# A two-layer encoder trunk: the odd layer's side work in woven streams of steps, and two recurrence chains that take their steps together

## Chip, cores and metric

One core of one Trainium2 chip runs the whole program in one launch. The metric is device time in microseconds (us), the median of several runs. The kernel before takes 2757.74 us, the median of 3 runs (2757.59 to 2758.05).

## What is computed

Two consecutive encoder layers over a sequence of 2048 rows of 1024 columns, fp32. The even layer mixes neighbourhood attention with a gated recurrence (GLA); the odd layer, which the change is mostly about, mixes HGRN2 heads with Mamba-2 (SSD) heads. Cut to the odd layer:

```python
def layer(x, c):                                   # both layers
    h = x * (1.0 + scale) + shift                  # from c
    y = odd_mixer(h, ...)                          # or even_mixer
    return layer_norm(ALPHA * x + gate * y)
def odd_mixer(h, w_in, ...):
    cq, cf_f, cf_b, ci, cg, dz, dxbc, dt_f, dt_b = split_cols(h @ w_in)
    # HGRN2: 4 heads of 128, forward and backward
    lf = logaddexp(log(lb), log1p(-lb) + log_sigmoid(cf)); k = (1 - lb) * sigmoid(-cf)
    oc = bidir_gated_recurrence(cq * 128 ** -0.5, ci, k_f, lf_f, k_b, lf_b)
    yc = rms_norm(oc) * silu(cg)
    # SSD: 8 heads of 64, 2 groups with a state of 128
    xs, bm, cm = split_cols(silu(conv1d(dxbc, conv_w, width=4) + conv_b))
    dt = softplus(dt_raw + dt_bias); a = dt * -exp(a_log)
    y = ssd(xs * dt_f, a_f, bm, cm) + rev(ssd(rev(xs * dt_b), rev(a_b), rev(bm), rev(cm))) + d_skip * xs
    yd = rms_norm(y * silu(dz))
    return concatenate([yc, yd]) @ w_out
```

## The kernel before

**In-projection.** Every fp32 product is made of three fp32r matmuls (high part by high, low by high, high by low: `hH,wh`, `hL,wh`, `hH,wl`). The in-projection of the odd layer goes unit by unit of 256 weight columns: `ci0 ci1` (values), `qf0` to `qf3` (queries and forward gates), `b0 b1` (backward gates), `x0` to `x3` (the input of the convolution), `g0 g1` and `dz0 dz1` (output gates). Each is done for the second half of the sequence ("half 1"), then for the first ("half 0"). `InProj.block` (matmuls in L205) is 24 matmuls into one PSUM bank: 128x512 in most units, 128x256 in `ci` and `dz`. The evacuations write an `st` tile on ACT or DVE (L348 to L354 for the first kind, L371 and L372 for the second), and DMAs store it to DRAM; `loading` (L184 to L186) loads and splits the next weights.

**Side work of the odd layer, per segment of 512 rows.**
- `Rec.pass_a` (L441 to L567) is the local part of one HGRN2 head: it loads the gates (`Kp`, L652), takes their sigmoid on ACT (`F`, L654), then goes through seven levels, on each of which PE makes 16 small `fine` matmuls (`blocks`, L435) or an `l` one (L498), DVE multiplies `Q` and `Kp` (L508, L510), POOL multiplies the other half of `Kp` (L512). Then come transposes `pk` (L527), the state updates `pu` (L538), a scan on DVE (L579) and the outputs `po` (L556, L561). Its generator yields 12 or 13 times. `pass_b` (L584 to L638, called `other`) adds the second direction for two heads.
- `Ssd.conv` (L1016 to L1043) filters one of 8 channel blocks: load `cvx` (L1027), one ACT pass (L1029), three DVE passes over `cva` (L1031), a sigmoid (ACT, L1032), a product (POOL, L1033); blocks below 6 are turned on PE (`cvt`, L1039), copied on ACT (L1041) and stored as rows of `xtok` (L1042).
- `Ssd.backward` (L1045) runs a chain of 16 chunks from the last to the first. For each: store the state `sb` (L1051), load `tk` from `xtok` (L1054), weight it on POOL (L1065), two PE matmuls `pu` (L1069), decay the state on POOL (L1077), add `pu` on DVE (L1078).
- `Ssd.steps` (L975) makes the decays from `dt_raw`.

**What sets the order.** A list scheduler orders all instructions ahead of time by priority, which is the order in which the program writes them; each engine then runs its list in order. In `trunk` the side work is written whole between `units(...)` calls, each piece inside `tc.high_priority(offset=2000)`, which moves its instructions ahead by 2000 places. Heads are taken one after another, and of a head the second segment (`sg` 2 half + 1) before the first. The even layer's GLA runs two chains through `lagging` (L309): chain a leads by 6 steps, after that `mixed` takes one step of each in turn. After the in-projection follow the SSD's `local` and `forward` parts with the out-projection (L1546 to L1568, matmuls `oo` in L921).

Of the kernel before, what the change touches and what calls it, by code (L numbers as in the profile page):

```python
# [10 lines left out]
F32 = mybir.dt.float32  # L11
# [296 lines left out]

def lagging(a, b, lag):  # L309

    for _ in range(lag):
        next(a)
        yield
    yield from mixed(a, b)


def chained(*gs):
    for g in gs:
        yield from g
# [627 lines left out]
class Ssd:  # L947
# [27 lines left out]
    def steps(self, pool, tp, bank, dt_raw, half):  # L975

        e, nc = self.e, self.e.nc
        n = NC // 2
        hs = slice(half * n, (half + 1) * n)
        dt = self.dt[:, hs]  # L980
        bc = lambda r: r.unsqueeze(1).broadcast_to([P, n, 16])
        z = tp[:, 0]
        nc.vector.tensor_tensor(z, dt_raw[:, hs], bc(self.row), ALU.add)
        ab = tp[:, 1]
        nc.scalar.activation(ab, z, AF.Abs)
        nc.scalar.activation(ab, ab, AF.Exp, scale=-1.0)
# [12 lines left out]
        nc.vector.scalar_tensor_tensor(dt, z, 0.0, h, ALU.max, ALU.add)
        a = z  # L1000
        nc.vector.tensor_tensor(a, dt, bc(self.nea), ALU.mult)
        nc.scalar.copy(self.aHr[:, hs], a)
        nc.vector.tensor_tensor(self.aL[:, hs], a, self.aH[:, hs], ALU.subtract)

        for nm, m, d in (("kf", "gt", 0), ("qf", "le", 0), ("kb", "lt", 1), ("qb", "ge", 1)):
            pt = bank("sp")
            nc.tensor.matmul(pt[:, :n * 8], e.tri[m], a[:, :, d * 8:(d + 1) * 8], start=True, stop=True)
            t = self.ed[nm][:, hs]
            nc.scalar.activation(t, pt[:, :n * 8].rearrange("p (c h) -> p c h", h=8), AF.Exp)
            if nm[0] == "k":  # L1010
                nc.vector.tensor_tensor(t, t, dt[:, :, d * 8:(d + 1) * 8], ALU.mult)
        pt = bank("sp")
        nc.tensor.matmul(pt[:, :n * 16], e.ones, a.rearrange("p c h -> p (c h)"), start=True, stop=True)
        nc.scalar.activation(self.tot[:, hs].rearrange("p c h -> p (c h)"), pt[:, :n * 16], AF.Exp)

    def conv(self, pool, bank, sg, xbc, cw, cb):  # L1016

        e, nc = self.e, self.e.nc
        t0 = sg * SW
        lo, hi = max(t0 - 2, 0), min(t0 + SW + 1, S)  # L1020
        for i in range(8):
# [23 lines left out]
    def backward(self, c, pool, bank):  # L1045

        nc = self.e.nc
# [4 lines left out]
        if c:  # L1052
            tk = pool.tile([P, 768], F32, name="tk", tag="tk", bufs=2)
            nc.sync.dma_start(tk, self.tok[c * P:(c + 1) * P, :])  # L1054
            pu = self.update(c, 1, tk, tk[:, 512:], pool, bank, tk[:, :512].rearrange("p (h q) -> p h q", h=8))
            new = pool.tile([P, 512], F32, name="sb", tag="sb", bufs=2)
            self.step(new, self.sb, c, 1, pu)
            self.sb = new

    def update(self, c, d, x, b, pool, bank, xw=None):  # L1060
# [59 lines left out]
    def forward(self, c, pool, bank):  # L1120
# [22 lines left out]
            nc.vector.tensor_tensor(h8(t), h8(po), eq, ALU.mult)  # L1143
            nc.gpsimd.tensor_tensor(acc, acc, t, ALU.add)
        if c < NC - 1:
            pu = self.update(c, 0, tk, tk[:, 512:], pool, bank)
# [66 lines left out]
def trunk(ctx, tc, i, out):  # L1213
# [246 lines left out]
        U[f"x{h}"]["evac"] = ch_evac(e, xbc[2 * h:2 * h + 2], [C, C], [1.0, 1.0])  # L1460
    recs = [Rec(e, mp, mps, [(0, P, cg[h], y[h * P:(h + 1) * P])], hg, 1.0, 1, f"h{h}") for h in range(4)]

    def hgrn(h, half):
        for sg in (2 * half + 1, 2 * half):
            with tc.high_priority(offset=2000):
                run(recs[h].pass_a(sg, hgrn_prep(e, mp, cq[h], cz[h], lb[:, h:h + 1], ub[:, h:h + 1]),
                                   v_loader(e, mp, ci[h // 2][:, (h % 2) * P:(h % 2 + 1) * P], P), sg % 2))

    sd = Ssd(e, sg_, dz, y[512:1024])

    def conv(sg):
        with tc.high_priority(offset=2000):
            sd.conv(kp, xbank, sg, xbc, cw, cbias)

    def back(sg):
        for c in range(4 * sg + 3, 4 * sg - 1, -1):
            with tc.high_priority(offset=2000):
                sd.backward(c, kp, xbank)

    def steps(half):  # L1480
        with tc.high_priority(offset=2000):
            sd.steps(sp, mp.tile([P, 4, NC // 2, 16], F32, name="dtt", tag="KT", bufs=1), xbank, dt_raw, half)

    def btags(t, par):
        return {"qul": (("F", "Kp")[t], 2), "stwb": ((("stw", "kd"), ("q", "KT"))[t][par], 1), "sq": (f"S32{t}", 1),
# [3 lines left out]
        return mps.tile([P, 512], F32, name=name, tag="rg" if name == "pob" else "sd", bufs=2)  # L1489

    def other(h, sg, tags=None):
        with tc.high_priority(offset=2000):
            run(pass_b(e, recs[h:h + 2], sg, mp, bbank, tags or [btags(t, sg % 2) for t in range(2)]))

    w1 = ip.load(U["b0"])
    for g in range(2):
# [5 lines left out]
    hgrn(0, 1)  # L1502
    units("qf1", 1)
    hgrn(1, 1)
    units("ci1 qf2 b1", 1)
    hgrn(2, 1)
    units("qf3", 1)
    hgrn(3, 1)
    units("x0 x1 x2 x3", 1)
    sd.prepare(sp, i["dt_bias"], i["a_log"], i["d_skip"])  # L1510
    steps(1)
    conv(3)
    back(3)
    units("g0 g1", 1)
    run(ip.turn(U["dz0"], U["dz1"], 1, U["qf0"], U["b0"], 0, lambda n: mp.tile([P, 4, 2 * P], F32, name="xt", tag=f"T{n % 2}", bufs=1), banks(mps, "rg", 2)))
    units("ci0", 0)
    hgrn(0, 0)
    units("qf1", 0)
    hgrn(1, 0)
    units("g0 ci1", 0)  # L1520
    steps(0)
    units("x0 x1 x2 x3", 0)
    for sg in range(4):
        other(0, sg)
    conv(2)
    back(2)
    conv(1)
    units("qf2", 0)
    back(1)
    units("b1", 0)  # L1530
    conv(0)
    units("qf3", 0)
    hgrn(2, 0)
    hgrn(3, 0)
    back(0)
    units("g1", 0)
    late = []
    late.append((U["dz0"], ip.load(U["dz0"])))
    run(ip.blocks(*late[-1], 0, 0))
    late.append((U["dz1"], ip.load(U["dz1"])))  # L1540
    run(ip.blocks(*late[-1], 0, 0))
    other(2, 0)
    for u, w in late:
        run(ip.blocks(u, w, 0, 1))
# [17 lines left out]
    for c in range(NC):  # L1562
        if 0 < c < NC - 1:
            sd.local(c + 1, mp, sbank)
        if c % 4 == 1 and c < 12:
            other(2, c // 4 + 1, ftags)
# [63 lines left out]
```

## Time and profile before

| what | value |
|---|---|
| median of 3 runs | 2757.74 us |
| the profiled execution | 2761.07 us, of it in the span 2759.3 us |
| PE busy, its weight loads (PEld) | 94%, 77% of the span |
| DVE, ACT, POOL busy | 52%, 40%, 47% |
| chain that ended last, by engine | PE 64%, DVE 12%, DMA 10%, ACT 5%, issue 4%, POOL 4% |
| even layer | 0 to 1394.6 us |
| odd layer to the first `g1` matmul of half 0 | 1394.6 to 2237.8 us |
| its `g1` and `dz` units of half 0 | 2237.8 to 2362.8 us |
| change-over | 2362.8 to 2415.9 us |
| SSD outputs and out-projection | 2415.9 to 2759.3 us |

The profiled execution lies 1.8 us above its own span and 3.3 us above the median. The stretches are cut at the first `oqf0` matmul, the first `g1` matmul of half 0, the end of the last `dz` matmul and the first `oo` matmul. A busy PE is not PE at its peak, since matmuls are pipelined. The trace shows each plain fp32 matmul (the small ones) as two records.

### The profile page before, as it was taken

How to read it: one execution, taken by the hardware profiler on the slowest of the kernel's cores; microseconds unless marked ns; L12 is line 12 of the kernel's file. 1: busy time of each engine (PE TensorE's matmuls, PEld its weight loads, DVE VectorE, ACT ScalarE, POOL GpSimd, SP SyncE). 2: the span in 40 equal slices, each digit the busy share in tenths (PEclk: the TensorE clock that was granted, in tenths of full speed). 3: DMA queues.
4: the chain of work that ended last, by engine and by line, in shares of the span. 5: the costliest groups of instructions: out<-in, count | busy, mean ns of one | idle time of the engine just before them, and what ended most of it. 6: DMA issues, size and time to landing. Idle time of an engine off the chain costs nothing.

```text
span 2759.3 us, 52948 instructions
## 1 busy us (share of the span) xinstructions
PE 2585.7 (94%) x21112; PEld 2122.1 (77%) x21112; DVE 1425.6 (52%) x2343; ACT 1107.0 (40%) x2317; POOL 1302.2 (47%) x1289
## 2 busy tenths in 40 slices
PE   7999798999999999999899999999999988788988
PEld 5878687987878677777788877888787768676876
DVE  6223335124442545554545445453545468778987
ACT  3152333155344533343232333353334344645643
POOL 4252324244442434343355555244535487577775
PEclk9999999999999779999999999999999999898999
DMA  8535434323365554545455334353346666544341
GB/s 272 166 107 166 139 122 139 106 90 114 118 224 178 192 176 154 180 151 157 134 179 198 112 120 142 112 184 126 118 140 219 191 187 220 191 138 140 100 133 68
DMA packets 260999, 420.92 MB, mean 153 GB/s; under 512 B 21232, under 2 KB 138896, under 8 KB 260752
## 3 DMA queue, kind: packets, MB, share of 16 engines
q1 hardware_dynamic: 260752, 417.53, 47.1%
q8 instruction: 167, 2.74, 0.4%
q14 instruction: 80, 0.66, 0.1%
HBM read 285.07 MB, written 132.38 MB: 151 GB/s over the span
## 4 chain that ended last, share of the span: by engine, by line
PE 64%; DVE 12%; DMA 10%; ACT 5%; issue 4%; POOL 4%; SPq 1%; POOLq 0%; DVEq 0%; ACTq 0%
PE oo L921 9%; PE ox L205 5%; PE oqf L205 5%; PE nay L825 4%; DMA adw<-in_ada_w_dram 3%; PE nas L802 3%; PE obv L205 3%; PE oag L205 3%; PE oav L205 3%; PE oak L205 3%; PE og L205 2%; PE fine L435 2%; PE napt L818 2%; PE oci L205 2%; DVE w L1115 2%
## 5 line engine op out<-in xcount | busy, mean ns | idle before, releaser
L186 POOL TENSOR_TENSOR wl<-wraw,wh 128x1024 fp32r<-128x1024 f32 (+2 forms) x116 | 291.8, 2533 | 313.4 <-ACT wh L185 308.8
L921 PE MATMUL oo<-wo,yH 128*128 128x512 f32 x1024 | 326.3, 405 | 6.6 <-ACT yH L905 4.7
L512 POOL TENSOR_TENSOR Kp<-Kp,T 128x256 f32<-128x256 f32 x144 | 118.6, 824 | 238.6 <-PE l L498 70.0
L921 PEld LDWEIGHTS oo<-wo,yH 128*128 128x128 f32 x1024 | 192.4, 192 | 50.4 <-ACT yH L905 7.5
L921 PE MATMUL oo<-wo,yL 128*128 128x512 f32 x512 | 200.4, 406 | 1.9 <-DVE yL L906 1.8
L815 POOL TENSOR_TENSOR nap<-nap,nasm 128x384 f32<-128x384 f32 (+2 forms) x128 | 110.9, 896 | 188.7 <-DVE nasm L810 152.8
L185 ACT CAST wh<-wraw 128x1024 fp32r<-128x1024 f32 (+2 forms) x116 | 116.8, 1051 | 158.0 <-PE obqk L205 25.8
L510 DVE TENSOR_TENSOR Kp<-Kp,T 128x256 f32<-128x256 f32 x144 | 106.6, 740 | 122.0 <-PE fine L435 59.3
L508 DVE TENSOR_TENSOR Q<-Q,T 128x512 f32<-128x512 f32 x144 | 140.9, 979 | 0.0
L825 PE MATMUL nay<-napts,nav 128*64 128x128 f32 (+1 forms) x896 | 134.8, 299 | 2.7 <-DVE napts L821 2.1
L825 PEld LDWEIGHTS nay<-napts,nav 128*64 128x64 f32 (+1 forms) x896 | 104.8, 148 | 36.8 <-issue 25.4
L1031 DVE SCALAR_TENSOR_TENSOR cva<-cvx,cw,cva 128x512 f32<-128x512 f32 x96 | 90.2, 952 | 62.3 <-ACT cva L1029 60.9
L921 PEld LDWEIGHTS oo<-wo,yL 128*128 128x128 f32 x512 | 98.1, 192 | 26.5 <-DVE yL L906 4.4
L473 DVE COPY_PREDICATED S<-lmask,fine 128x128 f32<-128x128 int32 x160 | 43.8, 298 | 122.6 <-PE fine L435 122.2
L205 PE MATMUL oqf<-hH,wh 128*128 128x512 f32 x256 | 102.5, 401 | 4.9 <-ACT st L353 4.9
L205 PE MATMUL oqf<-hH,wl 128*128 128x512 f32 x256 | 102.0, 399 | 0.0
L205 PE MATMUL ox<-hL,wh 128*128 128x512 f32 x256 | 101.9, 398 | 0.0
L205 PE MATMUL ox<-hH,wl 128*128 128x512 f32 x256 | 101.8, 398 | 0.0
L205 PE MATMUL oqf<-hL,wh 128*128 128x512 f32 x256 | 101.8, 398 | 0.0
L205 PE MATMUL ox<-hH,wh 128*128 128x512 f32 x256 | 101.7, 397 | 0.0
L807 ACT ACTIVATE nap<-nap,namx 128x384 f32<-128x384 f32 (+2 forms) x128 | 79.3, 620 | 54.6 <-DVE namx L805 53.4
L805 DVE CUSTOM_DVE_ANT_0 nap<-nas,nat 128x384 f32<-128x384 f32 (+2 forms) x128 | 70.4, 557 | 51.8 <-PE napt L818 33.0
(377 smaller groups left out, 7657.5 us busy)
## 6 DMA issues: line engine op xcount, KB each, us to landing
wraw<-in_o_w_dram SPq DMA_DIRECT2D x56, 512.0 KB
wraw<-in_e_w_dram SPq DMA_DIRECT2D x44, 512.0 KB
adw<-in_ada_w_dram SPq DMA_DIRECT2D x32, 512.0 KB
tk<-xtok SPq DMA_DIRECT2D x31, 384.0 KB
nat<-in_na_tab_dram SPq DMA_DIRECT2D x16, 640.0 KB
xt<-in_x_dram SPq DMA_DIRECT2D x16, 512.0 KB
adw<-in_ada_p_dram SPq DMA_DIRECT2D x16, 512.0 KB
r<-in_x_dram SPq DMA_DIRECT2D x16, 512.0 KB
```

The source lines that it names most:

```text
L185: nc.scalar.copy(h[:, sl], raw)
L186: (nc.vector if e.wl_dve else nc.gpsimd).tensor_sub(l[:, sl], raw, h[:, sl].bitcast(F32))
L205: nc.tensor.matmul(oo, a, b, start=d == 0 and m == 0, stop=d == ND - 1 and m == 2)
L508: nc.vector.tensor_tensor(qv, qv, view(tcur, toff + 1, [[nb - 1, 2], [2, n2], [0, s]]), ALU.mult)
L510: nc.vector.tensor_tensor(kv, kv, view(tcur, toff + nb + 1, [[2, n2], [0, s]]), ALU.mult)
L512: nc.gpsimd.tensor_tensor(kv, kv, view(tcur, toff, [[2, n2], [0, s]]), ALU.mult)
L802: nc.tensor.matmul(sc[:, :nk], a[sl, qs], b[sl, ks[0], ks[1]], start=m == 0, stop=m == 2, tile_position=(p0, 0))
L807: nc.scalar.activation(p[:, :nk], p[:, :nk], AF.Exp, bias=mx[:, n:n + 1], scale=-1.0, accum_out=sm[:, n:n + 1])
L815: nc.gpsimd.tensor_tensor(p[:, :nk], p[:, :nk], sm[:, n:n + 1].broadcast_to([P, nk]), ALU.mult)
L825: nc.tensor.matmul(yp[sl, n, :], vs[:4 * w, n, b, p0:p0 + 64], pts[:4 * w, b, :], start=b == 0, stop=b == nb - 1, tile_position=(0, p0))
L921: nc.tensor.matmul(o, a[:, c, :], b[c][:, ns], start=c == order[0] and m == 0, stop=c == order[-1] and m == 2)
L1031: nc.vector.scalar_tensor_tensor(acc, xr[:, k:k + SW], cw[:, i, k:k + 1], acc, ALU.mult, ALU.add)
```

## The change

1. `lagging` lets its two chains take a step each in one go and then yields twice (which keeps the number of yields); before, `mixed` yielded between them.
2. A new `woven(front, *streams)` runs the projection's steps and, whenever the number of front steps reaches a stream's due count (`first`, then every `per`), one step of that stream. In the odd layer the recurrences are one stream and the SSD's steps, convolution and backward chain another. `high_priority` is gone.
3. `hgrn` takes a list of heads and runs the two segments of a half as two chains through `lagging`, 6 steps apart.
4. `conv` takes several segments and goes block by block through all of them; a block's transposes and stores come one item late. Of `backward`, the weighting and the update become two steps. The tile `dtt` moves to another pool.
5. The order of units in half 0 is now `ci0 qf1 ci1 g0 qf2 b1 qf3 x0 x1 x2 x3 g1`, then `dz`; before, the `x` units stood ahead of `qf2`. In half 1 the order of units stays.

```diff
 def lagging(a, b, lag):
     for _ in range(lag):
         next(a)
         yield
-    yield from mixed(a, b)
+    alive = [a, b]
+    while alive:
+        for g in list(alive):
+            if next(g, alive) is alive:
+                alive.remove(g)
+        yield
+        if len(alive) == 2:
+            yield
...
+def woven(front, *streams):
+    due = [first for _, first, _ in streams]
+    for j, _ in enumerate(front):
+        for x, (g, _, per) in enumerate(streams):
+            while due[x] <= j:
+                due[x] += per
+                next(g, None)
+    for g, _, _ in streams:
+        run(g)
...
+        for i in range(8):
+            for sg in sgs:
+                done.append(filtered(i, sg))
+                if len(done) > 1:
+                    put(*done.pop(0))
+                yield
+        put(*done.pop(0))
+        yield
...
-            pu = self.update(c, 1, tk, tk[:, 512:], pool, bank, tk[:, :512].rearrange("p (h q) -> p h q", h=8))
+            xw = self.weighted(c, 1, tk, pool, tk[:, :512].rearrange("p (h q) -> p h q", h=8))
+            yield
+            pu = self.update(xw, tk[:, 512:], bank)
...
-    def hgrn(h, half):
-        for sg in (2 * half + 1, 2 * half):
-            with tc.high_priority(offset=2000):
-                run(recs[h].pass_a(sg, hgrn_prep(e, mp, cq[h], cz[h], lb[:, h:h + 1], ub[:, h:h + 1]),
-                                   v_loader(e, mp, ci[h // 2][:, (h % 2) * P:(h % 2 + 1) * P], P), sg % 2))
+    def hgrn(hs, half):
+        def chain(sg):
+            for h in hs:
+                yield from recs[h].pass_a(sg, hgrn_prep(e, mp, cq[h], cz[h], lb[:, h:h + 1], ub[:, h:h + 1]),
+                                          v_loader(e, mp, ci[h // 2][:, (h % 2) * P:(h % 2 + 1) * P], P), sg % 2)
+        return lagging(chain(2 * half + 1), chain(2 * half), Rec.STEPS // 2)
...
+    woven(chained(steps_of("qf1 ci1 qf2 b1 qf3 x0 x1 x2 x3 g0 g1", 1), turn),
+          (hgrn(range(4), 1), 0, 2), (chained(steps(1), conv(3), back(3)), 90, 8))
     units("ci0", 0)
...
+    def last():
+        yield from steps_of("qf1 ci1 g0 qf2 b1 qf3 x0 x1 x2 x3 g1", 0)
...
+        for nm in ("dz0", "dz1"):
+            late.append((U[nm], ip.load(U[nm])))
+            yield from ip.blocks(*late[-1], 0, 0)
+        for u, w in late:
+            yield from ip.blocks(u, w, 0, 1)
+    woven(last(), (chained(hgrn(range(2), 0), *(other(0, sg) for sg in range(4)), hgrn(range(2, 4), 0), other(2, 0)), 0, 2.15),
+          (chained(steps(0), conv(2, 1, 0), back(2, 1, 0)), 122, 2.67))
```

Three places show how the lists of the engines move.

On PE, in the unit `qf2` of half 1, a recurrence's `fine` and `pu` matmuls stood in turn, one by one, in the list before:

```order
L205 MATMUL oqf_15289<-hL,wh 128x512
L205 MATMUL oqf_15289<-hH,wl 128x512
L205 MATMUL oqf_15289<-hH,wh 128x512
L435 MATMUL fine<-Q,km 32x32 x10
L538 MATMUL pu<-v,KT 128x128
L435 MATMUL fine<-Q,km 32x32
```

and so on, `fine` and `pu` by turns, 14 pieces in all. Now they stand in runs, with projection matmuls (`oqf`) between them:

```order
L548 MATMUL pk<-c_ident,Kp 128x128 x8
L205 MATMUL oqf_14815<-hH,wl 128x512
L205 MATMUL oqf_14815<-hH,wh 128x512
L456 MATMUL fine<-Q,F 32x32 x16
L559 MATMUL pu<-v,KT 128x128 x4
L205 MATMUL oqf_14815<-hL,wh 128x512
```

From the first `oqf0` matmul to the first `g1` of half 0, the changes from one kind of small matmul to another fall from 145 to 76 (those between `fine` and `pu` or `po` from 98 to 19), and the visits from the projection to small matmuls rise from 139 to 146. The counts of matmuls stay.

On ACT, before, in the units `b1` and `qf3` of half 0: the sigmoids of head 2's gates (`F<-Kp`) stand ahead of an evacuation (`st<-ob`) of the unit `b1`, which makes those heads' backward gates:

```order
L1029 ACTIVATE cva<-cvx,cbias,cw 128x512 x2
L1041 COPY cvtt<-cvt 128x512
L1032 ACTIVATE cvx<-cva 128x512
L654 ACTIVATE F<-Kp 128x512 x2
L185 CAST wh<-wraw 128x1024 x2
L353 ACTIVATE st<-ob_21431 128x512
```

Now the sigmoids of head 2 stand in the `x` units, after the units `b1` and `qf3`:

```order
L1037 ACTIVATE tot<-sp 128x128
L648 ACTIVATE sq,ss<-opl 128x128 x2
L675 ACT_TABLE_LOAD
L675 ACTIVATE F<-Kp 128x512 x2
L676 ACTIVATE Kp<-Kp 128x1024
L1071 COPY cvtt<-cvt 128x512
L1056 ACTIVATE cva<-cvx,cbias,cw 128x512
L374 ACTIVATE st<-ox_20897 128x512
```

Nothing of the projection that still makes gates of head 2 stands behind them any more.

On PE in the `dz` units of half 0, steps of the backward chain (`pu<-tk`) were three before, the first of them here:

```order
L205 MATMUL odz_23010<-wl,hH 128x256
L205 MATMUL odz_23010<-wh,hL 128x256
L435 MATMUL fine<-kd,q 32x32 x3
L1069 MATMUL pu<-tk 128x256 x2
L435 MATMUL fine<-kd,q 32x32 x4
```

Now eleven stand there, all within the last 290 rows of PE's list of those units, in pairs that are 3 to 18 rows apart:

```order
L456 MATMUL fine<-Q,F 32x32 x9
L1115 MATMUL pu<-tk 128x256 x2
L582 MATMUL po<-stw,Q 128x128 x3
L582 MATMUL po<-ca,Q 128x128
L456 MATMUL fine<-Q,F 32x32 x7
L205 MATMUL odz_22578<-wh,hH 128x256
```

From the first `g1` matmul to the first `oo`, the 15 weighted steps of the backward chain number 7 before and 11 now (the other 4 stand in half 1 in both). On the other engines the same stretch of the lists has, before and now: on DVE 22 and 39 filter passes (L1031), 24 and 21 products of `Kp`, 27 and 23 of `Q`; on POOL 8 and 13 products of the convolution (L1033) and 24 and 21 of `Kp`. The recurrences have 25 groups of 16 `fine` matmuls in it before and 20 now.

## Rows read from the trace of the kernel before

**Rows 1.** Stretches: length, busy us of PE, PEld, DVE, ACT, POOL; PE clock, DMA share, GB/s.

```profile
1394.60:2237.80 843.20, 817.81 (x7107) 684.16 (x7106) 404.28 (x630) 325.67 (x593) 408.60 (x408) 1.00 0.48 156
2237.80:2362.80 125.00, 111.94 (x1469) 97.97 (x1467) 96.97 (x147) 57.58 (x114) 87.29 (x99) 0.99 0.58 190
2362.80:2415.90 53.10, 36.61 (x208) 30.04 (x208) 44.19 (x82) 37.47 (x113) 33.21 (x34) 0.76 0.65 220
2415.90:2759.30 343.40, 302.58 (x1444) 247.02 (x1444) 279.86 (x405) 171.61 (x482) 234.99 (x234) 0.95 0.36 115
```

**Rows 2.** What PE waited for, 1394.6 to 2237.8: us, times, longest.

```profile
PE oqf L205 <- ACT st L353: 4.9, 1, 4.9
...
PE odz L205 <- DVE st L372: 3.4, 3, 2.6
```

**Rows 3.** Timeline of PE, mixed matmuls in `qf2` of half 1: start, us.

```profile
1547.30 0.49 PE L538 MATMUL pu<-v,KT 128*128 128x128 f32 x2
1547.72 0.25 PE L435 MATMUL fine<-Q,km 128*32 128x32 f32 x2
1547.90 0.49 PE L538 MATMUL pu<-v,KT 128*128 128x128 f32 x2
```

**Rows 4.** Timeline of PE, the same matmuls in runs, `dz` of half 0.

```profile
2352.99 1.05 PE L538 MATMUL pu<-v,KT 128*128 128x128 f32 x8
2353.79 0.36 PE L205 MATMUL odz<-wh,hH 128*128 128x256 f32 x1
2354.09 0.46 PE L435 MATMUL fine<-Q,km 128*32 128x32 f32 x32
2354.48 1.16 PE L538 MATMUL pu<-v,KT 128*128 128x128 f32 x8
```

**Rows 5.** Timeline of ACT, `b1` and `qf3` of half 0.

```profile
2212.23 1.15 ACT L654 ACTIVATE F<-Kp 128x512 f32<-128x512 f32 x2 [3.69 <-DMA Kp<-cz]
```

**Rows 6.** Two short stretches, columns as in rows 1.

```profile
1395.00:1405.50 10.50, 10.50 (x48) 8.61 (x46) 8.32 (x17) 5.15 (x8) 7.82 (x9) 1.00 0.62 188
...
2216.40:2219.60 3.20, 3.20 (x9) 2.46 (x8) 2.77 (x2) 3.20 (x6) 3.20 (x3) 0.50 0.43 141
```

**Rows 7.** What PE waited for, 2237.8 to 2415.9.

```profile
PE pu L1069 <- POOL tk L1065: 3.5, 4, 2.2
...
PE py L1131 <- DVE opl L621: 2.2, 1, 2.2
```

**Rows 8.** Groups of DVE and POOL, 1395 to 2420: busy us, mean ns.

```profile
L1031 DVE SCALAR_TENSOR_TENSOR cva<-cvx,cw,cva 128x512 f32<-128x512 f32 x96 | 90.2, 952 | 62.3 <-ACT cva L1029 60.9
L1078 DVE TENSOR_TENSOR sb<-sb,pu 128x512 f32<-128x512 f32 x15 | 10.2, 683 | 15.0 <-POOL sb L1077 15.0
L508 DVE TENSOR_TENSOR Q<-Q,T 128x512 f32<-128x512 f32 x96 | 96.7, 1008 | 0.0
L510 DVE TENSOR_TENSOR Kp<-Kp,T 128x256 f32<-128x256 f32 x96 | 72.6, 757 | 73.9 <-PE fine L435 39.0 <-ACT km L468 16.3 <-PE l L498 15.5
L1033 POOL TENSOR_TENSOR cva<-cva,cvx 128x512 f32<-128x512 f32 x32 | 45.6, 1430 | 55.9 <-ACT cvx L1032 47.5 <-PE po L561 3.3 <-issue 3.0
L512 POOL TENSOR_TENSOR Kp<-Kp,T 128x256 f32<-128x256 f32 x96 | 77.7, 810 | 137.2 <-PE l L498 49.6 <-ACT km L468 35.2 <-ACT F L468 24.0
L1065 POOL TENSOR_TENSOR tk<-tk,edkb 128x512 f32<-128x512 f32 x15 | 19.1, 1274 | 9.4 <-DMA tk<-xtok 9.4
L1077 POOL TENSOR_TENSOR sb<-sb,tot 128x512 f32<-128x512 f32 x15 | 17.0, 1131 | 8.0 <-ACT tot L1014 3.1 <-DMA sbd<-sb 1.9 <-DVE sb L1078 1.6
```

**Rows 9.** The `fine` matmuls alone, 2237.8 to 2362.8: length, PE, PEld.

```profile
2237.80:2362.80 125.00, 12.91 (x768) 9.57 (x768) 0.99 0.58 190
```

**Rows 10.** Timeline of POOL: a wait for the load of a backward step.

```profile
2166.40 1.04 POOL L1065 TENSOR_TENSOR tk<-tk,edkb 128x512 f32<-128x512 f32 x1 [5.18 <-DMA tk<-xtok]
```

**Rows 11.** What PE waited for, 60 to 1395 (even layer).

```profile
PE oak L205 <- DVE st L348: 16.7, 4, 7.3
```

More of the change, by code (lines that the diff above doesn't have):

```diff
@@ L1014, in steps, with conv, filtered @@
         nc.scalar.activation(self.tot[:, hs].rearrange("p c h -> p (c h)"), pt[:, :n * 16], AF.Exp)
-    def conv(self, pool, bank, sg, xbc, cw, cb):
+        yield
+    def conv(self, pool, bank, sgs, xbc, cw, cb):
         e, nc = self.e, self.e.nc
-        t0 = sg * SW
-        lo, hi = max(t0 - 2, 0), min(t0 + SW + 1, S)
-        for i in range(8):
+        done = []
+        def filtered(i, sg):
+            t0 = sg * SW
+            lo, hi = max(t0 - 2, 0), min(t0 + SW + 1, S)
             xr = pool.tile([P, SW + 4], F32, name="cvx", tag="cvx", bufs=e.cv_bufs)
@@ L1033, in conv, with put @@
             nc.gpsimd.tensor_tensor(acc, acc, xr[:, 0:SW], ALU.mult)
+            return i, t0, acc
+        def put(i, t0, acc):
             if i >= 4:
@@ L1043, in conv @@
                                   tt.rearrange("p (c n) -> p c n", c=SC))
+        for i in range(8):
[3 more added lines that the diff above has]
+                    put(*done.pop(0))
+                yield
+        put(*done.pop(0))
+        yield
     def backward(self, c, pool, bank):
@@ L1054, in backward @@
             nc.sync.dma_start(tk, self.tok[c * P:(c + 1) * P, :])
-            pu = self.update(c, 1, tk, tk[:, 512:], pool, bank, tk[:, :512].rearrange("p (h q) -> p h q", h=8))
+            xw = self.weighted(c, 1, tk, pool, tk[:, :512].rearrange("p (h q) -> p h q", h=8))
+            yield
+            pu = self.update(xw, tk[:, 512:], bank)
             new = pool.tile([P, 512], F32, name="sb", tag="sb", bufs=2)
@@ L1058, in backward, with weighted @@
             self.sb = new
-    def update(self, c, d, x, b, pool, bank, xw=None):
+        yield
+    def weighted(self, c, d, x, pool, xw=None):
         nc = self.e.nc
@@ L1066, in update @@
                                 ed[:, c, :].unsqueeze(2).broadcast_to([P, 8, 64]), ALU.mult)
+        return xw
+    def update(self, xw, b, bank):
+        nc = self.e.nc
         pu = bank("pu")
@@ L1145, in forward @@
         if c < NC - 1:
-            pu = self.update(c, 0, tk, tk[:, 512:], pool, bank)
+            pu = self.update(self.weighted(c, 0, tk, pool), tk[:, 512:], bank)
             new = pool.tile([P, 512], F32, name="sf", tag=f"{'kq'[c % 2]}m0", bufs=1)
@@ L1461, in trunk, with conv, back @@
     recs = [Rec(e, mp, mps, [(0, P, cg[h], y[h * P:(h + 1) * P])], hg, 1.0, 1, f"h{h}") for h in range(4)]
-    def hgrn(h, half):
-        for sg in (2 * half + 1, 2 * half):
-            with tc.high_priority(offset=2000):
-                run(recs[h].pass_a(sg, hgrn_prep(e, mp, cq[h], cz[h], lb[:, h:h + 1], ub[:, h:h + 1]),
-                                   v_loader(e, mp, ci[h // 2][:, (h % 2) * P:(h % 2 + 1) * P], P), sg % 2))
-    sd = Ssd(e, sg_, dz, y[512:1024])
[L1471 to L1478, printed above, removed]
+    def hgrn(hs, half):
[4 more added lines that the diff above has]
+        return lagging(chain(2 * half + 1), chain(2 * half), Rec.STEPS // 2)
+    sd = Ssd(e, sg_, dz, y[512:1024])
+    def conv(*sgs):
+        return sd.conv(kp, xbank, sgs, xbc, cw, cbias)
+    def back(*sgs):
+        for sg in sgs:
+            for c in range(4 * sg + 3, 4 * sg - 1, -1):
+                yield from sd.backward(c, kp, xbank)
     def steps(half):
-        with tc.high_priority(offset=2000):
-            sd.steps(sp, mp.tile([P, 4, NC // 2, 16], F32, name="dtt", tag="KT", bufs=1), xbank, dt_raw, half)
+        return sd.steps(sp, kp.tile([P, 4, NC // 2, 16], F32, name="dtt", tag="cvt", bufs=1), xbank, dt_raw, half)
     def btags(t, par):
@@ L1491, in other @@
     def other(h, sg, tags=None):
-        with tc.high_priority(offset=2000):
-            run(pass_b(e, recs[h:h + 2], sg, mp, bbank, tags or [btags(t, sg % 2) for t in range(2)]))
+        return pass_b(e, recs[h:h + 2], sg, mp, bbank, tags or [btags(t, sg % 2) for t in range(2)])
     w1 = ip.load(U["b0"])
@@ L1501, in trunk @@
     units("ci0", 1)
[L1502 to L1509, printed above, removed]
-    sd.prepare(sp, i["dt_bias"], i["a_log"], i["d_skip"])
[L1511 to L1515, printed above, removed]
-    units("ci0", 0)
[L1517 to L1544, printed above, removed]
+    sd.prepare(sp, i["dt_bias"], i["a_log"], i["d_skip"])
+    turn = ip.turn(U["dz0"], U["dz1"], 1, U["qf0"], U["b0"], 0,
+                   lambda n: mp.tile([P, 4, 2 * P], F32, name="xt", tag=f"T{n % 2}", bufs=1), banks(mps, "rg", 2))
+    woven(chained(steps_of("qf1 ci1 qf2 b1 qf3 x0 x1 x2 x3 g0 g1", 1), turn),
+          (hgrn(range(4), 1), 0, 2), (chained(steps(1), conv(3), back(3)), 90, 8))
+    units("ci0", 0)
+    def last():
+        yield from steps_of("qf1 ci1 g0 qf2 b1 qf3 x0 x1 x2 x3 g1", 0)
+        late = []
+        for nm in ("dz0", "dz1"):
[5 more added lines that the diff above has]
+          (chained(steps(0), conv(2, 1, 0), back(2, 1, 0)), 122, 2.67))
     closed("pp1", "sp1", "wa1")
@@ L1565, in trunk @@
         if c % 4 == 1 and c < 12:
-            other(2, c // 4 + 1, ftags)
+            run(other(2, c // 4 + 1, ftags))
         op.tile(c, (4, 8), c == NC - 1, sd.forward(c, mp, sbank))
```

## The prediction

> **What bounds the kernel now.** I read the stretches first, then what PE waited for in each, then timelines around the waits. Up to the first `g1` matmul of half 0 the odd layer hangs on PE: it is busy 817.81 of 843.2 us, DVE and POOL less than half of that [rows 1]. So a microsecond of PE's own work that goes there comes off the end, and so does one of the 25.4 us in which PE stands idle. From there to the first `oo` matmul the picture turns: PE idles 13.1 us of 125.0 and 16.5 of 53.1, while DVE works (96.97 + 44.19) of 178.1 us, 79%, and POOL (87.29 + 33.21), 68% [rows 1]. In the last stretch DVE leads with 279.86 of 343.4 us, and PE's matmuls wait for it. Nothing of computation is added or taken away: what can change is the order of PE's matmuls, who waits for whom, and how much side work is left for the end.
>
> **Part 1: PE's small matmuls in runs.** In the mixed piece a pair of `pu` and a pair of `fine` records take 1547.30 to 1547.90, that is 0.60 us [rows 3]. In runs, 8 `pu` take 2352.99 to 2353.79 and 32 `fine` 2354.09 to 2354.48 [rows 4], so the same two pairs would take 0.20 + 0.02 = 0.22. The difference, 0.38 us for two changes of kind, makes 0.19 a change. The lists lose 145 - 76 = 69 such changes before the `g1` unit: 69 x 0.19 = -13.1 us. Seven more visits from the projection cost, at the same 0.19, +1.3. All of it lies on the engine that is busy 97% there. Bounds: 0, if something else then sets the pace, and -13.1; I take the full value, because PE's idle time there is small.
>
> **Part 2: waits that go.** Head 2's sigmoids stand on ACT behind their load, idle 3.69 us at 2212.23 [rows 5], and ahead of an evacuation that PE needs; PE stands 4.9 us for it, once [rows 2]. Now these sigmoids come when the gates have long been stored: -4.9. After that wait the granted clock is 0.50 of full speed, the 1.2 GHz level, for 3.20 us [rows 6], which costs half of that: -1.6. The 3.4 us for which `dz` matmuls of half 1 wait for their evacuation [rows 2] come from filter passes ahead of it on DVE; the convolution of that half is now spread over the `x` units and later ones: -3.4. Sum -9.9; bounds 0 (each load and filter pass may meet another evacuation that PE needs) and -9.9. I take all of it: of the 25.4 us of idle time there [rows 1] these are the two largest pieces with side work as their cause, and the lists show both causes gone from in front of those evacuations.
>
> **Part 3: eleven backward steps at the end.** Seven stood in the end stretch, eleven stand there now. Their PE waits were 3.5 us there [rows 7], 0.5 a step; eleven make 5.5: +2.0. Each step is queued on all of SP (store and load), POOL (two passes), PE and DVE; a `pu` that waits holds back every projection matmul behind it. Bounds: nothing, and 2.2 a step, the longest wait seen [rows 7]; the load alone has kept POOL idle for 5.18 [rows 10], and that is kept for a rival.
>
> **Part 4: density of the end stretch.** By the lists and the means of rows 8: DVE gets 17 more filter passes (x 0.952 = +16.2) and 4 more `sb` sums (+2.7), and loses 4 `Q` (-4.0) and 3 `Kp` products (-2.3): +12.6 us. POOL gets 5 products (x 1.430 = +7.2), 4 `tk` (x 1.274 = +5.1) and 4 `sb` (x 1.131 = +4.5), and loses 3 `Kp` (-2.4): +14.4. Against it, the recurrences' chain is shorter: 20 groups of `fine` instead of 25, where 768 records of 32 a group make 24 groups in 125.0 us [rows 9], 5.2 us each. If the added work falls into idle time, nothing; if it comes on top at the stretch's own density, +12.6 / 0.79 = +15.9 or +14.4 / 0.68 = +21.2; if the chain sets the end, 5 x 5.2 = -26. I take 0, since DVE has 37 us of idle time there and no engine is full, and keep both ends.
>
> **Part 5: the rest.** In the even layer the two chains only change how their steps interleave; its large wait, 16.7 us in 4 [rows 11], stays, since DVE there stands behind weight loads that aren't touched. I take 0; one wait of the mean 4.2 more, or most of one less, bounds it: -3 to +4. In the last stretch `other` loses its priority in three places; three waits of 2.2 [rows 7] bound it at +-6.6, and I take 0, because DVE's work there stays the same.
>
> **A rule against it.** PE is busy 843.2 - 25.4 us there, but that is not how full it is: weight loads take 684.16 [rows 1], 81%, and 8.61 of 10.50, 82%, in a run of 48 projection matmuls [rows 6]. The Trainium skill, "Perfetto Trace Analysis", section Identifying the Most-Contended Engine, says that the share of matmul time is a poor measure of how near TensorE is to its roof, and that the share of weight loads is the one to use; by that the stretch could shrink only to 684.16 / 0.82 = 834, some 9 us instead of the 21.7 that parts 1 and 2 make, and the time would be 2751. I keep the 21.7, since the two sides of its first term were timed for the same small matmuls [rows 3, 4], and the 82% are those of wide ones.
>
> **Sum.** -13.1 + 1.3 - 9.9 + 2.0 = -19.7. Against the profiled execution 2761.1 - 19.7 = 2741.4; that execution lies 3.3 above the median, so **2738 us**. Its own range is 2728 to 2748 (the even layer, the last stretch and half of parts 1 and 2).
>
> **Rivals.**
> - *The end gets denser.* Part 4 on top at +15.9 (DVE) to +21.2 (POOL): 2754 to 2759. For it: both engines are over two thirds busy there, and the `tk` pass takes 1.04 us alone [rows 10] but 1.274 in the mean [rows 8]. Against it: no engine is full, and the recurrences ask for less. The Trainium skill, "GPSIMD Engine Reference", section 1 Specifications, says that GpSimd shares its SBUF interfaces with VectorE, with contention when a DVE instruction reads two SBUF inputs; the filter passes do so, and the mean above the lone duration agrees.
> - *The end gets shorter*, because the recurrences' chain paces it: 2738 - 26 = 2712.
> - *The backward steps hold PE* (slower). Eleven steps in the last `dz` units, by the lists 290 rows of PE, must each be loaded, weighted, multiplied and added one after another; PE waits in order at each `pu`. Halfway between 2.2 and 5.18, at 3.7 us a step, they cost 40.7 - 3.5 = 37.2 instead of 2.0: 2773. The wait per step decides: gains of 21.7 are eaten at (21.7 + 3.5) / 11 = 2.3, and it is slower by 0.2% from 2.8. Against it: only one wait of seven steps reached 2.2.
> - *It doesn't do what it says on the path*: changes between kinds were covered by the recurrences' own pace, and other evacuations are late instead: 2758. Against it: PE stands idle only 3% of that time [rows 1].
>
> **How the numbers follow.** A difference of 0.2%, 5.5 us, is about what a measurement of this kernel can tell from none. Forecast 0.46, shorter end 0.13, denser end 0.20, PE held 0.14, nothing 0.07. Faster by over 0.2% (below 2752.2): the first two and a fourth of the denser end, 0.64. Within: the rest of that case, less a little, and nothing happening, 0.20. Slower: PE held and the top of the denser end, 0.16. The range goes from 2712, the shorter end, to 2768, short of most of the case in which PE is held.
>
> **What would show it.** In the profile after, the stretch from the first `oqf0` to the first `g1` of half 0 should take some 821 us (843.2 - 21.7), with no PE wait behind ACT of several us and `fine` records in rows of 32; the units stand in another order, so the stretch ends at the same matmul count. The stretch from there to the first `oo` should stay at 178 (+ 2), with waits of `pu` (backward) of some 5 us. A first stretch of 835 or more makes part 1 wrong; an end stretch of 194 or more, with DVE or POOL near 80%, is the denser end; waits of 20 us or more behind `tk` are the rival that holds PE; 152 or so is the shorter end.

## The result: slower, 2802 us

The changed kernel takes 2802.06 us (median of 4 runs, 2796.33 to 2806.28), the kernel before 2757.69 beside it; ratio 1.0157 [1.0137, 1.0178]. The forecast of 2738 and its range up to 2768 are missed, and the sign too. The profiled execution's span is 2801.6 us, 42.3 above [rows 1]'s kernel. Stretches of the changed kernel, with the columns of [rows 1], cut at the same matmuls; first `oqf0` to first `g1` of half 0, then to the first `oo`, then the end:

```profile
1403.80:2235.30 831.50, 812.95 (x7247) 682.15 (x7245) 400.75 (x624) 318.70 (x588) 410.31 (x414) 0.99 0.47 150
2235.30:2427.80 192.50, 155.74 (x1533) 132.97 (x1531) 155.68 (x233) 99.29 (x232) 132.81 (x127) 0.89 0.65 217
2427.80:2801.60 373.80, 310.08 (x1448) 255.94 (x1448) 286.48 (x406) 172.09 (x482) 232.20 (x233) 0.90 0.33 106
```

The same of the kernel before, now cut exactly at its first `oo` (2413.2; [rows 1] cuts 2.7 us later):

```profile
2237.80:2413.20 175.40, 147.27 (x1674) 127.33 (x1672) 138.51 (x225) 95.06 (x226) 118.65 (x131) 0.92 0.60 198
2413.20:2759.30 346.10, 303.86 (x1448) 247.69 (x1448) 282.52 (x409) 171.61 (x482) 236.84 (x235) 0.95 0.36 116
```

| stretch | before | after | difference | forecast |
|---|---|---|---|---|
| even layer | 1394.7 | 1403.8 | +9.1 | 0 |
| first `oqf0` to first `g1` of half 0 | 843.1 | 831.5 | -11.6 | -21.7 |
| to the first `oo` | 175.4 | 192.5 | +17.1 | +2.0 |
| last stretch | 346.1 | 373.8 | +27.7 | 0 |

The cut at `g1` is at the same projection matmul, but not at the same side work: in the changed kernel 140 more of PE's records stand ahead of it, five groups of `fine` (160 records) less some others. The first `ci0` matmul of half 0 and the first `oo` cut at equal counts, to a record. Between them stand, for half 1 and then half 0, before:

```profile
1394.70:1908.10 513.40, 503.02 (x4472) 421.66 (x4471) 236.85 (x362) 189.62 (x324) 238.06 (x241) 1.00 0.45 147
1908.10:2413.20 505.10, 461.96 (x4308) 389.74 (x4306) 305.84 (x491) 231.11 (x496) 289.09 (x297) 0.97 0.55 179
```

and after:

```profile
1403.80:1909.30 505.50, 498.05 (x4473) 419.59 (x4471) 235.59 (x363) 188.96 (x324) 243.54 (x241) 1.00 0.46 150
1909.30:2427.80 518.50, 470.64 (x4307) 395.53 (x4305) 320.85 (x493) 229.03 (x496) 299.58 (x300) 0.95 0.54 175
```

So the weave gains 7.9 us in half 1 and loses 13.4 in half 0, and up to `g1` it gains about half of what was forecast. The largest loss lies in the last stretch, where every engine has nearly the same work as before (PE 1448 records, DVE 406 instead of 409) and the diff changes one call, which runs three times. There `local` makes the weights `w` of a chunk in eight DVE passes, `sf` is the running state that the matmuls `pin` read, `yacc` the output sum that the transposes `pt` turn, and `syo` closes an output tile. What PE waited for there, in the changed kernel:

```profile
PE pin L1185 <- DVE sf L1124: 26.7, 7, 9.3
PE pt L1204 <- ACT yacc L1201: 15.3, 3, 12.2
```

In the kernel before the first two were 9.6 and 5.9 us:

```profile
PE pin L1139 <- DVE sf L1078: 9.6, 7, 2.0
PE pt L1158 <- ACT yacc L1155: 5.9, 3, 2.8
```

DVE's timeline of the changed kernel ahead of the longest `pt` wait (start, us), and the PE row that waits:

```profile
2597.16 4.71 DVE L1161 SCALAR_TENSOR_TENSOR w<-c_t_ge,dt,w 128x128 f32<-128x128 f32 x6
...
2601.91 0.56 DVE L1161 SCALAR_TENSOR_TENSOR w<-c_t_ge,dt,w 128x128 f32<-128x128 f32 x2
...
2607.62 5.63 DVE L1161 SCALAR_TENSOR_TENSOR w<-c_t_ge,dt,w 128x128 f32<-128x128 f32 x8
...
2614.37 0.67 DVE L1124 TENSOR_TENSOR sf<-sf,pu 128x512 f32<-128x512 f32 x1
...
2615.89 1.51 DVE L1196 TENSOR_TENSOR yacc<-yacc,dzl 128x512 f32<-128x512 f32 x1 [0.25 <-POOL yacc L1190]
```

```profile
2619.18 1.12 PE L1204 MATMUL pt<-c_ident,yacc 128*128 128x128 f32 x4 [12.19 <-ACT yacc L1201]
```

The sixteen `w` passes of two chunks' `local` parts stand within 16 us, and the state sum `sf` and the output sum `yacc` of the tile in work come behind them. Counting the `w` passes in DVE's list between the closing passes `syo` of neighbouring output tiles gives, before, 8 0 8 16 8 0 8 8 16 0 8 8 8 0 0; after, 8 0 16 0 16 0 16 0 16 0 16 0 8 0 0. I call the second list **paired**: all `w` passes of two tiles stand in one of them, time after time.

### The profile page after: what moved, and what is told of

It is laid out like the page before. It is cut to its first block, busy times and chain, and to the rows that moved or that the text cites. A ratio compares the mean times of both kernels' runs of the same rounds, so it can differ in the third digit from the quotient of the medians.

```text
span 2801.6 us, 52962 instructions
## 1 busy us (share of the span) xinstructions
PE 2591.0 (92%) x21112; PEld 2134.9 (76%) x21112; DVE 1450.2 (52%) x2343; ACT 1106.6 (39%) x2317; POOL 1306.3 (47%) x1289
## 4 chain that ended last, share of the span: by engine, by line
PE 42%; DVE 10%; DMA 6%; issue 3%; ACT 3%; POOL 2%; SPq 0%; POOLq 0%; DVEq 0%; ACTq 0%
PE oo L942 10%; PE oqf L205 6%; PE nay L846 4%; PE ox L205 3%; PE ob L205 3%; PE nas L823 2%; PE og L205 2%; DVE w L1161 2%; PE odz L205 2%; PE oci L205 2%; PE napt L839 2%; DVE cva L1058 2%; PE fine L456 1%; DMA cvx<-xbc 1%; PE pin L1185 1%
## 5 line engine op out<-in xcount | busy, mean ns | idle before, releaser
L529 DVE TENSOR_TENSOR Q<-Q,T 128x512 f32<-128x512 f32 x144 | 147.2, 1022 | 0.0
L1058 DVE SCALAR_TENSOR_TENSOR cva<-cvx,cw,cva 128x512 f32<-128x512 f32 x96 | 99.6, 1053 | 41.7 <-ACT cva L1056 38.7
L156 POOL TENSOR_TENSOR hL<-hf,hH 128x512 fp32r<-128x512 f32 x36 | 50.4, 1407 | 100.4 <-ACT hH L155 100.2
```

The lines of the kernel that those rows point to most:

```text
L529: nc.vector.tensor_tensor(qv, qv, view(tcur, toff + 1, [[nb - 1, 2], [2, n2], [0, s]]), ALU.mult)
```

## Experiments

Theory P: the pairing costs the last stretch. Rival Q: the priority that `other` lost there does. Rival G: it is all GLA. In the table "to g1", "to oo" and "last" are the stretches above, in us, from each run's profile. Ratios are to the kernel before, measured beside the run on the same chip (2759.7 us beside runs 1 to 4, 2761.1 beside 5 to 8, 2755.9 beside 9 to 12, 2757.4 beside 13 and 14), so medians of different groups compare only through them.

| run | even | to g1 | to oo | last | list | median | ratio |
|---|---|---|---|---|---|---|---|
| before | 1394.7 | 843.1 | 175.4 | 346.1 | not | 2757.7 | 1 |
| after | 1403.8 | 831.5 | 192.5 | 373.8 | paired | 2802.1 | 1.0157 [1.0137, 1.0178] |
| 1 | 1405.9 | 832.0 | 192.2 | 370.2 | paired | 2799.8 | 1.0154 [1.0116, 1.0191] |
| 2 | 1395.0 | 834.9 | 191.4 | 339.2 | not | 2756.9 | 0.9993 [0.997, 1.0017] |
| 3 | 1399.4 | 843.2 | 177.0 | 341.7 | not | 2759.6 | 1.0007 [0.9991, 1.0024] |
| 4 | 1400.2 | 843.8 | 183.6 | 338.0 | not | 2767.4 | 1.0038 [1.0019, 1.0057] |
| 5 | 1390.4 | 828.6 | 193.1 | 372.5 | paired | 2790.7 | 1.0114 [1.0081, 1.0146] |
| 6 | 1402.1 | 828.9 | 190.8 | 347.9 | not | 2774.4 | 1.0047 [1.0032, 1.0061] |
| 7 | 1394.1 | 830.5 | 186.3 | 367.6 | paired | 2779.1 | 1.0065 [1.0039, 1.009] |
| 8 | 1390.4 | 842.5 | 182.8 | 339.7 | not | 2760.3 | 0.9993 [0.9978, 1.0008] |
| 9 | 1389.0 | 829.6 | 184.3 | 329.3 | not | 2738.2 | 0.9933 [0.9915, 0.9952] |
| 10 | 1391.6 | 828.3 | 185.9 | 358.8 | first part | 2764.3 | 1.0033 [1.0019, 1.0046] |
| 11 | 1394.7 | 845.7 | 176.6 | 334.6 | not | 2749.1 | 0.9974 [0.9959, 0.9988] |
| 12 | 1390.8 | 840.0 | 189.0 | 349.8 | not | 2768.9 | 1.0046 [1.0031, 1.0061] |
| 13 | 1389.0 | 843.7 | 175.4 | 340.8 | not | 2752.8 | 0.9978 [0.9965, 0.9991] |
| 14 | 1389.7 | 831.1 | 185.8 | 329.7 | not | 2741.9 | 0.9936 [0.9915, 0.9957] |

The first `oo` is not a fixed point: run 4 has 8.2 us more ahead of it than the kernel before and 8.1 less behind it. So a few us between "to oo" and "last" are one stretch's as much as the other's.

**Run 1: the priority back in the last stretch.**

```diff
-            run(other(2, c // 4 + 1, ftags))
+            with tc.high_priority(offset=2000):
+                run(other(2, c // 4 + 1, ftags))
```

> The changed kernel with the priority given back to the three pass_b calls of the last stretch, nothing else. The profile of the changed kernel is longer than before by 27.7 us after the first oo matmul. Theory P (the lists): DVE's list there has the eight w passes of two chunks behind each other (16, 0, 16, 0 per output tile, where before it was 8, 0, 8, 16, 8, 0, 8, 8), and the state sums and yacc behind them come late; this kernel keeps that pairing, so it stays at 2802 (within 6). Rival Q (the priority itself): the pass_b work comes too late without it; then 2802 - 28 = 2774.

2799.8 us: theory P. The last stretch is 370.2 with the priority and 373.8 without.

**Run 2: and GLA in turn.**

```diff
-        return lagging(chain(0), chain(1), Rec.STEPS // 2)
+        return inturn(chain(0), chain(1), Rec.STEPS // 2)   # yield from mixed(a, b), as before
```

> The kernel of the first run, and GLA's two chains again in turn as before. By its lists the pairing in the last stretch is gone (8, 0, 8, 8, 16, 0, 8, 8). Theory P: the last stretch back at 346, -28, and if the even layer's +9.1 came from the chains' steps, -9 more: 2765. Rival Q: 2765 too, but then the first run was at 2774. If the even layer's loss has another cause: 2774.

2756.9, lower than expected. The even layer is back and so is the last stretch, though the edit touches only the even layer: it turned the list of the last stretch, some 1700 us after GLA's recurrences. The end from `g1` to `oo` stays at 191.4.

**Run 3: the kernel before without the priority in the last stretch** (`other` there is run bare).

> The kernel before, with the priority taken from the three pass_b calls of the last stretch alone. Its lists there aren't paired (8, 0, 8, 8, 16, 0, 8, 8). Theory P: 2758 (within 5). Rival Q: 2758 + 28 = 2786.

2759.6: rival Q falls.

**Run 4: the kernel before with the new `lagging`.**

> The kernel before, with the new way of taking the two chains' steps, which there only GLA in the even layer uses. If the even layer's +9.1 us comes from it: 2767. If not: 2758.

2767.4 us, as expected. Its profile has in the even layer waits of PE that the kernel before has not, or less of (`fine` behind `Q` was 3.1 there):

```profile
PE fine L442 <- DVE Q L515: 6.2, 3, 3.0
PE oag L205 <- ACT st L360: 5.6, 2, 3.5
...
PE fine L442 <- ACT F L475: 3.7, 1, 3.7
```

Profiles of kernels with the old steps have the even layer at 1389.0 to 1399.4, those with the new ones (after, 1, 4, 6) at 1400.2 to 1405.9. The nearest of these lie 0.8 us apart; it is the ratio of run 4 that shows the loss, 0.4%, some 10 us, by its interval 5 to 16. Some 8 us fit both.

**Run 5: the changed kernel with GLA in turn** (as in run 2, without run 1's edit).

> The changed kernel with GLA's two chains in turn as before; no priority in the last stretch. By its lists the w passes there are paired (16, 0, 16, 0), which they are not in the second run's kernel, whose only other difference is the priority in three places. Theory P (the pairing costs the last stretch): the even layer back (-8), the last stretch at about 372: 2794. Rival G (GLA's order in the even layer is behind all 43 us that the second run gave back): 2757.

2790.7: rival G falls. Runs 2 and 5 have the same order in the even layer; their last stretches are 339.2 and 372.5, and PE's wait of `pin` for `sf` is 10.4 in run 2 and, in run 5,

```profile
PE pin L1192 <- DVE sf L1131: 26.9, 7, 9.3
```

The two differ in the priority alone, so here it is the priority that turns the list. That the priority by itself is not the cause rests on runs 1 and 3: with it and paired 370.2, without it and not paired 341.7.

**Run 6: the changed kernel, its output tiles 40 places ahead.**

```diff
-        op.tile(c, (4, 8), c == NC - 1, sd.forward(c, mp, sbank))
+        with tc.high_priority(offset=40):
+            op.tile(c, (4, 8), c == NC - 1, sd.forward(c, mp, sbank))
```

> The changed kernel, GLA and all else as it is, with each output tile of the last stretch moved 40 places ahead in priority, which by the lists undoes the pairing (8, 0, 8, 8, 16, 0, 8, 8). Theory P: the last stretch back at 340 to 346, 2802 - 28 = 2774. Rival G: 2802.

2774.4. Its last stretch, from the first `oo` to the end, with the `sf` wait at 6.9 us:

```profile
2421.80:2769.70 347.90, 304.17 (x1448) 248.06 (x1448) 287.97 (x406) 172.59 (x482) 229.76 (x233) 0.95 0.35 114
```

DVE's busy time is that of the changed kernel (286.48); 26 us went with the order alone, 20 of them PE's idle time (63.7 to 43.7) and 6 its busy time at a granted clock of 0.95 instead of 0.90. Not all of it need be the pairing: run 13 puts the 40 places on a list that isn't paired, and its last stretch is 5 us shorter than before.

**Run 7: half 1 woven, half 0 and the last stretch as before.** Here and in runs 9 to 12 and 14, "as before" means the order and the priorities; point 4 of the change (a block's transposes one item late, the backward step in two) stays in.

```diff
-    woven(last(), (chained(hgrn(range(2), 0), ...
+    alone(0, 0)            # the code of before, each piece with priority
+    units("qf1", 0)
...
```

> Only half 1 of the odd layer in woven streams; half 0 and the last stretch in the order and with the priorities of before, GLA in turn. By its lists the w passes of the last stretch are paired all the same. From the first oqf0 to the first ci0 matmul of half 0: 505 us as in the changed kernel (513 before), if the runs of small matmuls and the missing evacuation waits act there by themselves. From the first g1 of half 0 to the first oo: 176 as before, if the denser end comes from the weave of half 0. Theory P: the last stretch 372, time 2758 - 8 + 28 = 2778. Rival G: 2750.

2779.1. Half 1 takes 505.1 us, as expected. From `g1` to `oo` it is 186.3, not 176: only part of the denser end belongs to half 0's weave.

**Run 8: convolution and backward steps earlier in half 0.**

```diff
-        yield from steps_of("qf1 ci1 g0 qf2 b1 qf3 x0 x1 x2 x3 g1", 0)
+        yield from steps_of("qf1 ci1 g0 qf2 b1 x0 x1 x2 x3 qf3 g1", 0)
...
-          (chained(steps(0), conv(2, 1, 0), back(2, 1, 0)), 122, 2.67))
+          (chained(steps(0), conv(2, 1, 0), back(2, 1, 0)), 106, 2.67))
```

> The kernel of the second run (priority in the last stretch, GLA in turn) with unit qf3 of half 0 behind the x units and the stream of convolution and backward steps 16 steps of the projection earlier (first 106 instead of 122): some six of the convolution's items, 18 filter passes of 1.05 us, leave the stretch from g1 to oo. By its lists the last stretch isn't paired. If DVE's amount of work sets that stretch: 191 - 18 = 173, time 2757 - 18 = 2739. If the recurrences' chain sets it, or head 3, whose gates come later now: 191 or more, 2757 or more.

2760.3: the time of the second branch, but the stretch fits neither. DVE's work from `g1` to `oo` fell from 156.89 us in run 2 to 139.54, and the stretch by 8.6, but the stretch before it grew by 7.6: from the first `ci0` of half 0 to `oo` run 2 takes 520.0 and run 8 519.8, where the kernel before takes 505.1. So DVE's amount at the very end is not what half 0 pays for. DVE's busy time over the whole of half 0 the edit left as it was (323.30 and 321.91 us, 305.84 in the kernel before), so run 8 says nothing against that.

**Run 9: run 7 with run 6's edit.**

> The kernel of the seventh run (half 1 woven, half 0 as before, GLA in turn) with the output tiles of the last stretch 40 places ahead, which undoes the pairing there. Theory P: the last stretch 345 instead of 368, 2779 - 23 = 2756 with the seventh run's 186 from g1 to oo; if that stretch, too, goes back to the 176 of before, 2746. It is the version that should beat both kernels: the weave where it pays and nowhere else. If the seventh run's loss was not the pairing: 2779.

2738.2, ratio 0.9933 [0.9915, 0.9952]: faster than both kernels, and by more than the 2746 to 2756 expected, for the last stretch came to 329 and not 345. Half 1, half 0 to `oo`, last stretch:

```profile
1389.00:1893.30 504.30, 496.76 (x4473) 418.88 (x4472) 239.05 (x363) 188.84 (x324) 242.78 (x241) 1.00 0.46 150
1893.30:2402.90 509.60, 463.69 (x4308) 391.23 (x4306) 304.12 (x494) 228.36 (x494) 291.25 (x300) 0.96 0.55 178
2402.90:2732.20 329.30, 298.45 (x1448) 246.97 (x1448) 276.51 (x406) 171.16 (x482) 233.78 (x233) 0.96 0.37 121
```

**Run 10: run 7 without the priority in the last stretch.**

> The kernel of the seventh run with the priority taken from the three pass_b calls of the last stretch. By its lists the w passes are then paired in the first four tiles only (8, 0, 16, 0, 16, 0, 8, 8, 8, 8, 9, 7). Theory P: taking the priority away makes this kernel faster, 2779 - 15 = 2764. Rival Q (the pass_b calls come late without it): 2779 or more.

2764.3: taking the priority away makes this kernel faster, by some 9 us (ratios 1.0065 and 1.0033, last stretch 367.6 and 358.8); the rest of the 15 us between the medians is between chips. With part of the pairing goes part of the loss (358.8, between 329 and 368).

**Run 11: of half 1, the two chains alone.**

```diff
+    woven(steps_of("qf1 ci1 qf2 b1 qf3 x0 x1 x2 x3", 1), (hgrn(range(4), 1), 0, 2))
+    prio(steps(1), conv(3), back(3))
+    units("g0 g1", 1)
```

> The kernel of the ninth run, but of half 1 the recurrences alone in the woven stream; steps, convolution and backward chain written whole with priority behind the x units, as before. It splits half 1's 7.9 us: if 5.0 of them are PE's own (the small matmuls in runs) and 3.0 the waits behind the convolution in the dz units, half 1 takes 513.4 - 5.0 = 508.4 here, and the time is 3 us above the ninth run's.

Half 1 takes 522.5 us: a miss, and of little use. The front has 160 steps, the recurrences' stream would need some 208 of them, so its rest was written as one piece ahead of the `g` units. Up to the first `x0` matmul, before the convolution comes in, it is 219.5 us in this run, 219.2 in the changed kernel and 222.5 before.

**Run 12: half 1 as before, half 0 woven, with run 6's edit.**

> Half 1 of the odd layer as before, half 0 woven as in the changed kernel, GLA in turn, the output tiles 40 places ahead (not paired). If the weave of half 0 costs what the second run shows (from its first ci0 to oo 520.0, 505.1 before): half 1 513.4, half 0 to oo 520, the last stretch 340 to 348, together 2768 to 2776. If the weave of half 0 costs only together with that of half 1: 2757.

2768.9. From the first `ci0` of half 0 (1905.1) to `oo` 514.7, 9.6 above the kernel before; half 0's weave loses without half 1's. Run 13 below is nearer to it, with the 40 places and half 1 as before: beside it run 12's ratio is 0.7% higher, some 19 us, 10.7 of them up to `oo` (504.0 there) and 9.0 behind it. In all profiles half 0 lies between 499.7 and 513.7 us in the order of before and between 513.7 and 520.0 woven.

**Run 13: the kernel before with run 6's edit. Run 14: run 9's kernel again.**

> The kernel before with the output tiles of the last stretch 40 places ahead, nothing else. Its lists there read like the ninth run's (8, 0, 8, 8, 16, 0, 8, 8). If the 40 places give the last stretch its 329 us: 2757 - 17 = 2740 less nothing from half 1. If they only undo the pairing, which the kernel before doesn't have: 2757 within 5, and the ninth run's gain is half 1's 8 to 9 us and the rest chance of the order.

> The ninth run's kernel again, on the same chip as run 13: 0.993 of the kernel before, 2738 if that is at 2757. It should be 8 to 9 us faster than run 13, half 1's share, if the two parts add.

2752.8 and 2741.9 beside 2757.4: the 40 places alone give 0.22% [0.09, 0.35], about 6 us, and run 14's kernel 11 more (the executions of the two, 2748.3 to 2757.9 and 2738.6 to 2745.7, do not overlap). In the profiles half 1 takes 515.1 and 505.3, which is 10 of it; up to `g1` run 14 is ahead by 12.6, to `oo` it is behind by 10.4, and in the last stretch ahead by 11.1, with lists that read alike there. Run 9's gain repeats (0.9936).

## Why the prediction was wrong

- **The last stretch (part 5)** is the step that failed. I bounded it by three waits of `other`, "because DVE's work there stays the same". The work did stay; its order did not. The two lists show the pairing (16, 0, 16, 0), and the prediction compares lists only up to the first `oo`. On an engine that is 82% busy and that PE waits for, equal work in another order cost 27.7 us: five lumps of sixteen passes of 0.7 us stand ahead of `sf` or `yacc`, two of them before waits of 9.3 and 12.2 us, the others before several of 3 to 4. One such lump is not enough: the kernel before has two, with no wait above 4.1 us beside them. Runs 1, 2, 5, 6, 7, 9 and 10 show it: not paired 329 to 350 in all kernels, paired 368 to 374, paired in its first part 359. How an edit in the even layer turns the list is the scheduler's doing and was not traced.
- **The even layer (part 5)** was bounded by -3 to +4 from one wait that stayed. Some +8 came; run 4 puts it on the way the steps are taken, and its profile shows new waits on `Q`, `F` and an evacuation. That these waits make up the whole is not shown.
- **The density of the end (part 4)** was taken at 0, with +15.9 as the rival's price; +17.1 came, with DVE at 81% (155.68 of 192.5; before 79%, 138.51 of 175.4): the denser end by the prediction's own sign. Run 8 shows, though, that this is no matter of DVE's amount there alone: taken out, it comes back in the stretch before. Run 12 puts 10 us or more on half 0's weave; runs 7, 9, 10 and 14, without it, still have 184 to 186 up to `oo`, run 11 177. What the sum of part 4 left out is that the passes themselves grow: over the whole of half 0 DVE is busy 318.6 to 323.3 us in every run with half 0 woven and 302.3 to 305.8 in every other, for about as many instructions (491 before, 493 after; see the last section). Whether this sets half 0's pace was not tested; it stays open.
- **PE's small matmuls in runs (part 1)**: right in kind, too large. In half 1 PE's busy time fell from 503.0 to 498.1 us, by 5.0, for 53 changes less and 9 visits more, 0.11 a change; run 9's half 1, with the same counts and the granted clock at full speed throughout, has 496.8, which makes 0.14. Part 1 took 0.19 from a single place [rows 3, 4]. Up to the first `g1` all of parts 1 and 2 brought -11.6 instead of -21.7. The sentence on weight loads, which allowed 9, was nearer: their share in the changed kernel is 682.15 of 831.5, 82%, as in a run of projection matmuls alone [rows 6]. The Trainium skill, "Perfetto Trace Analysis", section Identifying the Most-Contended Engine, names MFU (the share of the peak matmul rate) beside that share; the prediction leaves MFU out.
- **Waits that go (part 2)**: the 4.9 us behind head 2's sigmoids are gone from the list of waits, as is the wait of `dz` matmuls in half 1, where that unit pair went from 64.7 to 61.6 us, -3.1 where -3.4 was forecast. New waits took part of it: `fine` for `Q` 3.7, `sp` for `gt` 3.6. And the clock's -1.6 turned round: up to `g1` PE spent 3.4 us at the lower of its two levels (0.50, 1.2 GHz) before and 17.1 after (from 1693.1, 2150.5 and 2215.4), which by part 2's own half costs some 7 us more. Part of that is chance, since runs 3 and 13, with the order of before up to there, have 10.2.

```profile
PE fine L456 <- DVE Q L529: 3.7, 2, 3.4
```

- **The backward steps (part 3 and the slower rival)**: refuted. The eleven steps made PE wait 2.3 us in all, less than seven did before [rows 7].

```profile
PE pu L1115 <- POOL tk L1107: 2.3, 2, 1.6
```

The chance of slower, 0.16, hung on this and on the top of the denser end. The denser end came, but by its own price it makes 2754 to 2759; the last stretch, bounded at 6.6, is what leads past it.

## What to carry to other kernels

Where a scheduler writes the lists, compare them in every stretch, those that the diff doesn't touch too, and ask of the fullest engine not only how much work it has but what stands ahead of the passes that another engine waits for. Take a woven order apart by stretch before judging it: here half 1's weave gains 8 to 9 us, half 0's loses 10 to 19, GLA's 8, and a paired list some 26. A small priority on the work that ends a tile left the list not paired in all six kernels in which it was tried (runs 6, 9 and 11 to 14); two of them, the changed kernel and that of run 7, are paired without it.

## What was not expected of the hardware

DVE's passes grew longer as the end became denser: between `g1` and `oo` the filter pass took 985 ns in the mean before and 1077 after, though its shape is the same.

```profile
L1031 DVE SCALAR_TENSOR_TENSOR cva<-cvx,cw,cva 128x512 f32<-128x512 f32 x24 | 23.0, 985 | 5.3 <-ACT cva L1029 5.2
```

```profile
L1058 DVE SCALAR_TENSOR_TENSOR cva<-cvx,cw,cva 128x512 f32<-128x512 f32 x39 | 41.2, 1077 | 7.0 <-ACT cva L1056 7.0
```

POOL's share there rose only from 118.65 / 175.4 = 68% to 132.81 / 192.5 = 69%, so the share does not tell. Pass by pass the traces do. Of the 1536 filter passes in the sixteen profiles, 729 ran while no POOL instruction did, and each took 734 to 755 ns; the 807 with a POOL instruction beside them took 733 to 2971, 1199 in the mean, so every pass above 755 ns had one beside it. In half 0, 40 of 72 passes ran without one before, and they took 68.5 us in all; spread by the weave 19 do, and they take 79.9, which is 11 of the 15 us by which DVE's busy time grew there. The Trainium skill, "GPSIMD Engine Reference", section 1 Specifications, says that GpSimd and VectorE share their SBUF interfaces. The traces agree, though no run changes POOL's work alone.

In the last stretch the granted clock fell with the waits: 0.95 before, 0.90 paired, 0.95 in run 6, for the same matmuls; PE was busy 303.86, 310.08 and 304.17 us. It spent 37.9, 73.3 and 37.3 us there at the lower level (0.50, 1.2 GHz); beside the wait of 12.2 us that ends at 2619.18 that is from 2611.3 to 2625.0.
